# Hybrid block, one core: tiles that TensorE reads at one end of the SBUF, the rest at the other

## The chip, the core and the metric

The kernel runs on one core of a Trainium2 chip. A core has five engines with a queue each: TensorE (PE in the profile; its weight loads are PEld), VectorE (DVE), ScalarE (ACT), GpSimd (POOL) and SyncE (SP), which here only starts transfers. They share a 128-partition on-chip memory, the SBUF, and PE writes to a second one, the PSUM, in banks of 2 KB per partition. Each queue is worked in order; semaphores hold an instruction until others are done.

The metric is the device time of one call in microseconds (us), the median of several runs.

## The reference

One layer, for 1024 tokens of width 1024, all in float32:

```python
h = rms_norm(x, g_pre)
u = einsum('bsd,dn->bsn', h, w_in)             # 1024 x 8192: 10 blocks of 512, and 3*1024 merge logits
y_pool = pool_mixer(pool_v, ...) * silu(pool_g)     # causal means over 2, 4, 8, 16 tokens, then a 128x128 mix
y_conv = conv_mixer(conv_x, conv_gb, conv_gc, ...) * silu(conv_g)   # 3-tap causal convolution
y_sb = stick_breaking_attention(q, k, v) * silu(sb_g)               # 8 heads of 64
proj = einsum('bsnw,nwd->bsnd', branches, w_branch)  # three projections 512 -> 1024
merged = sum(sigmoid(merge) * proj, over the branches)
out = x + rms_norm(einsum('bsd,de->bse', merged, w_out), g_post)
```

In the attention a weight is sigmoid(logit) times the product of sigmoid(-logit) over all later keys, so each row needs a reversed running product (a scan) in place of a softmax.

## The kernel before, in words

Every operand of a product is held as two parts, a rounded high part and the rest (`hi`, `lo`), and a product is three matmuls: hi by hi, hi by lo, lo by hi. `split` (L72) makes the parts: a ScalarE copy (L73) and a subtraction on VectorE or GpSimd (L74). Weights are loaded in 128x512 pieces into `wraw` or `sraw`, split into the `w_hi` and `w_lo` tiles of the pool `wsp` (three of each, so up to two ahead), and used once.

Four stages follow each other.

1. To about 34 us: x is loaded, normed and transposed into `hh` and `hl`, four tiles each (two halves of the features by two halves of the tokens).
2. To about 332 us: the attention. `logits` (L366) multiplies queries with keys, takes two sigmoids (`sn`, `sp`, ScalarE), scans `sn` on VectorE (L386), and multiplies `sp` by the shifted `sn` on GpSimd (L388). `transposes` turns `sp` on PE, splits it into `wh` and `wl`; `values` (L408) multiplies with the values into `o`, adds a `low` half and writes `y_sb`. Between these steps `fillers` issues the blocks of the input product for the next heads (L189). The tile `tmp` takes the values before their transposition and the gates of this branch.
3. To about 936 us: everything else of the input product, in pairs of blocks by a seven-product scheme (`run_pair`, L564). It needs seven right-hand sides: three quarters of h as they are (`b11`, `b21`, `b22`), the quarter `b12` overwritten by a combination (`t4`), and three new combinations `t1`, `t2`, `t3`, each a pair of tiles (`t1h`, `t1l` and so on) of the pool `quarters`, built once by `build_quarters`. A product (L539) is 12 matmuls of 128x512. A pair takes the products b11, t2, b21, t3, t1, t4, b22 in this order, and there are 24 pairs. Between them stand the branch projections (`branch_proj`, L491; 24 matmuls per 128 outputs): of the attention first, with its parts in the pool `ysp` (L506), later of the other two with theirs in `ypp`. Partial sums are kept in DRAM (`proj_d`) and read back as `pr`; the merge gates and branch outputs are the tiles `g`, `sig`, `y`, `ph`, `pl` of the pool `gates`, the terms of a pair are `m1`, `u2`, `u3` of `tmps`.
4. To the end: the output product (L796), with the eight merged rows `m` as the stationary operand and the halves of w_out (`oh`, `wo`) moving, then the norm and the residual. The first four `m` were stored to DRAM and are read back (`taken_back`, L749) through the tiles `mr`; they go to the pool `fin`. The last four reuse `big`, the pool that held h.

A scheduler sets the order on each engine from the order of the code and its own estimates, and it inserts the waits. It also gives each pool its place: pools on the left are stacked upward from the low end of the SBUF, pools with `side="right"` downward from the high end, and a pool that is closed gives its room to later ones. With `reuse_waits="tile"` a tile that lies on old ones waits for the users of these alone. The right-hand stack of this build starts at byte 229,344 of a partition, which is 32 more than a multiple of 64; the left-hand tiles start at multiples of 64.

```python
bigp = op("big", KB)
tpool, close_t = pool_of("quarters", 6, side="right")
stp, close_stp = pool_of("stp", 2, side="right")
ysp, close_ysp = pool_of("ysp", 4, side="right")
held["m"] = op("fin", 1, side="right", reuse_waits="tile")
```

Of the kernel before, what the change touches and what calls it, by code (L numbers as in the profile page):

```python
# [8 lines left out]
F32 = mybir.dt.float32  # L9
# [5 lines left out]
P = 128  # L15
# [20 lines left out]
def hybrid_block_kernel(ctx, tc, x, g_pre, w_in, pool_w, pool_scale, conv_w, conv_b, w_branch, w_out, g_post, out):  # L36
# [17 lines left out]
    wraw = op("wraw", 3)  # L54
# [164 lines left out]
    ysb_pool = ysb_stack.enter_context(tc.tile_pool(name="ysb", bufs=4))  # L219
    qk_stack = ExitStack()  # L220
    qkp = qk_stack.enter_context(tc.tile_pool(name="qk", bufs=3))

    def tmp_tile():
        return qkp.tile([P, S], F32, tag="tmp", name="tmp", bufs=2)
# [96 lines left out]
    with tc.tile_pool(name="au", bufs=3) as au, \  # L321
            tc.tile_pool(name="wt", bufs=3) as wtp, tc.tile_pool(name="ps_z", bufs=2, space=PSUM) as ps_z, \
# [43 lines left out]
        def logits(p, s, i):  # L366
            n = (i + 1) * P
            q = ops["q", p][s]
            k, kl = ops["k", p][s]
            qs = slice(i * P, n)  # L370
            sp = au.tile([P, S], F32, tag="sp", name="sp", bufs=4)
            sn = au.tile([P, S], F32, tag="sn", name="sn", bufs=2)
            mid = (i + 1) // 2 * P if n > HALF else 0
            for c0, c1 in ((mid, n), (0, mid)):
                if c0 == c1:
                    continue
                w = c1 - c0
                z = ps_z.tile([P, HALF], F32, tag="z", name="z")
                nc.tensor.matmul(z[:, :w], q[:, qs], k[:, c0:c1], start=True, stop=False)  # L379
                if c1 == n:  # L380
                    nc.tensor.matmul(z[:, w - P:w], ident_r, mask_r, start=False, stop=False)
                nc.tensor.matmul(z[:, :w], q[:, qs], kl[:, c0:c1], start=False, stop=True)  # L382
                nc.scalar.activation(sn[:, c0:c1], z[:, :w], AF.Sigmoid, scale=-0.125)  # L383
                nc.scalar.activation(sp[:, c0:c1], z[:, :w], AF.Sigmoid, scale=0.125)  # L384
            rev = sn[:, 0:n][:, ::-1]
            nc.vector.tensor_tensor_scan(out=rev, data0=rev, data1=zeros.to_broadcast([P, n]), initial=1.0, op0=ALU.mult,  # L386
                                         op1=ALU.max)
            nc.gpsimd.tensor_tensor(out=sp[:, 0:n - 1], in0=sp[:, 0:n - 1], in1=sn[:, 1:n], op=ALU.mult)  # L388
            ops["w", p, s, i] = sp
# [18 lines left out]
        def values(p, s, i):  # L408
# [11 lines left out]
            low = au.tile([P, 2 * P], F32, tag="low", name="low", bufs=2)  # L420
# [76 lines left out]
    tpool, close_t = pool_of("quarters", 6, side="right")  # L497
# [7 lines left out]
    stp, close_stp = pool_of("stp", 2, side="right")  # L505
    ysp, close_ysp = pool_of("ysp", 4, side="right")  # L506
# [42 lines left out]
    held["raw"] = op("sraw", 5, reuse_waits="tile")  # L549
    held["sum"] = op("ssum", 3, reuse_waits="tile")  # L550
    for d in range(KB):
# [3 lines left out]
        if d % 2 == 0:  # L555
            build_quarters(d // 2)
    close_ysp()
    close_stp()
    tmps, close_tmps = pool_of("tmps", 1, side="right")
# [117 lines left out]
    gpool = op("gates", 4, reuse_waits="tile")  # L677

# [55 lines left out]
    def take_merged(d, ts, m):  # L734
        if d not in m_parts:
            o = (held["m"].tile([P, 2, S], F32R, tag="m", name="m", bufs=4) if d < 4
                 else bigp.tile([P, 2, S], F32R, tag="big", name="m"))
# [11 lines left out]
    def taken_back():  # L749

        for d in range(KB):
            if d < 4:
                m = held["m"].tile([P, S], F32, tag="mr", name="mr", bufs=2)
# [21 lines left out]
    close_tmps()  # L775
    close_t()
    held["m"] = op("fin", 1, side="right", reuse_waits="tile")
# [8 lines left out]
    fin = held["m"]  # L786
    gpost_sb = fin.tile([P, D], F32, tag="gpost", name="gpost_sb")
# [17 lines left out]
    def square(ps, var):  # L805
        junk = fin.tile([P, HALF], F32, tag="junk", name="junk")
# [92 lines left out]
```

## Time and profile before

| | us |
|---|---|
| median of 3 runs | 1033.36 (1031.94 to 1034.29) |
| profiled execution, its own time | 1032.51 |
| its span, first to last instruction | 1030.7 |
| outside the span | 1.8 |
| PE busy | 997.1, 4752 matmuls |
| mean granted TensorE clock | 0.997 of full |

The page of a profile lists the busy time of each engine, the chain of work that ended last, and the costliest groups of instructions by line. A group reads: line, engine, operation, written tile, read tiles, shapes, count, busy time, mean duration, idle time before, and what ended that idle time. In a matmul's row the moving operand stands first after the arrow and the stationary one second. The duration of a matmul runs to its modelled end, so matmuls overlap in such rows; what one costs in a row of them is the distance from one start to the next. In the chain a row reads: start, length, engine, written tile, line, count.

### The profile page before, as it was taken

What the parts mean: (1) busy time and instruction counts of PE and PEld (TensorE: products, weight loads), DVE (VectorE), ACT (ScalarE), POOL (GpSimd) and SP (SyncE); (2) the same over time, 40 slices, a digit from 0 to 9 for tenths busy, and PEclk for the clock granted to TensorE, in tenths of its full rate; (3) what the DMA queues carried; (4) which work ended last, traced back from release to release, by engine and by line L of the source; (5) the groups of instructions that cost most, each with busy time, mean ns of one, the idle gap of its engine ahead of it and who ended that gap; (6) DMA issues with size and microseconds to landing.
All of it is one profiled execution on the core that took longest, in us unless ns stands there. A gap on an engine that the chain in (4) does not pass through costs nothing.

```text
span 1030.7 us, 13275 instructions
## 1 busy us (share of the span) xinstructions
PE 997.1 (97%) x4752; PEld 825.0 (80%) x4752; DVE 636.5 (62%) x847; ACT 447.8 (43%) x871; POOL 453.0 (44%) x359
## 2 busy tenths in 40 slices
PE   4999999999998999999999999999999999999997
PEld 3788888888887788888888888888888888887886
DVE  6556766767776968889686685566333434465133
ACT  6557668668664553332232233343332322354111
POOL 3134543634564015455445444445555565556000
PEclk9999999999999999999999999999999999999999
DMA  6101000100101442322212224455434533256033
GB/s 227 60 21 35 28 22 22 41 21 21 31 22 31 163 153 62 98 66 72 83 52 72 82 62 163 153 191 167 133 126 125 209 112 120 65 186 223 1 123 123
DMA packets 43986, 97.09 MB, mean 94 GB/s; under 512 B 5264, under 2 KB 5520, under 8 KB 43920
## 3 DMA queue, kind: packets, MB, share of 16 engines
q1 hardware_dynamic: 43776, 95.71, 28.5%
q8 instruction: 38, 0.62, 0.2%
q10 hardware_dynamic: 144, 0.52, 0.1%
q14 instruction: 28, 0.23, 0.1%
HBM read 73.15 MB, written 23.07 MB: 93 GB/s over the span
## 4 chain that ended last, share of the span: by engine, by line
PE 84%; ACT 5%; DVE 4%; POOL 3%; issue 2%; DMA 2%; SPq 0%; POOLq 0%; DVEq 0%; ACTq 0%
PE g_ps L539 26%; PE q_ps L539 17%; PE g_ps L189 12%; PE pp L491 11%; PE o_ps L796 8%; PE o L418 3%; PE tp L404 2%; DVE sn L386 2%; PE z L382 1%; PE z L379 1%; POOL w_lo L74 1%; POOL sp L388 1%; ACT sn L383 1%; DMA xt<-in_x_dram 1%; ACT sp L384 1%
## 5 line engine op out<-in xcount | busy, mean ns | idle before, releaser
L74 POOL TENSOR_TENSOR w_lo<-s,w_hi 128x512 fp32r<-128x512 f32 x95 | 132.4, 1394 | 181.6 <-ACT w_hi L73 179.1
L388 POOL TENSOR_TENSOR sp<-sp,sn 128x127 f32<-128x127 f32 (+3 forms) x64 | 81.2, 1272 | 132.9 <-DVE sn L386 69.0
L74 POOL TENSOR_TENSOR w_lo<-s_raw,w_hi 128x512 fp32r<-128x512 f32 x70 | 94.2, 1346 | 96.5 <-ACT w_hi L73 92.3
L386 DVE TENSOR_TENSOR_SCAN sn<-sn,zeros 128x128 f32<-128x128 f32 (+3 forms) x64 | 100.5, 1574 | 48.3 <-ACT sn L383 45.5
L73 ACT CAST w_hi<-s 128x512 fp32r<-128x512 f32 x96 | 59.6, 621 | 136.0 <-PE g_ps L539 65.7
L73 ACT CAST w_hi<-s_raw 128x512 fp32r<-128x512 f32 x70 | 43.4, 620 | 132.5 <-PE g_ps L539 52.6
L189 PE MATMUL g_ps<-hh,w_hi 128*128 128x512 f32 x240 | 99.4, 414 | 0.3 <-ACT hh L285 0.3
L189 PE MATMUL g_ps<-hl,w_hi 128*128 128x512 f32 x240 | 94.5, 394 | 0.3 <-DVE hl L286 0.3
L189 PE MATMUL g_ps<-hh,w_lo 128*128 128x512 f32 x240 | 94.5, 394 | 0.0
L539 PE MATMUL g_ps<-hh,w_hi 128*128 128x512 f32 x236 | 92.6, 392 | 0.0
L539 PE MATMUL g_ps<-hh,w_lo 128*128 128x512 f32 x236 | 92.1, 390 | 0.0
L539 PE MATMUL g_ps<-hl,w_hi 128*128 128x512 f32 x236 | 91.8, 389 | 0.0
L74 POOL TENSOR_TENSOR w_lo<-w_raw,w_hi 128x512 fp32r<-128x512 f32 x44 | 67.6, 1535 | 53.1 <-ACT w_hi L73 53.1
L491 PE MATMUL pp<-yhi,w_lo 128*128 128x512 f32 x192 | 75.0, 392 | 0.7 <-DVE g L717 0.7
L491 PE MATMUL pp<-ylo,w_hi 128*128 128x512 f32 x192 | 75.0, 392 | 0.0
L491 PE MATMUL pp<-yhi,w_hi 128*128 128x512 f32 x192 | 74.9, 391 | 0.0
L383 ACT ACTIVATE sn<-z 128x384 f32<-128x384 f32 (+2 forms) x96 | 47.9, 499 | 29.7 <-PE z L382 20.4
L232 DVE TENSOR_TENSOR wl<-tp,wh 128x512 fp32r<-128x512 f32 (+2 forms) x96 | 50.4, 544 | 15.4 <-ACT wh L405 14.9
L539 PE MATMUL q_ps<-hh,w_hi 128*128 128x512 f32 x148 | 58.0, 392 | 0.0
L539 PE MATMUL q_ps<-hh,w_lo 128*128 128x512 f32 x148 | 57.9, 391 | 0.0
L539 PE MATMUL q_ps<-hl,w_hi 128*128 128x512 f32 x148 | 57.5, 389 | 0.0
L133 DVE TENSOR_TENSOR s<-s_raw 128x512 f32<-128x512 f32 x48 | 41.9, 873 | 23.4 <-POOL w_lo L74 22.8
(205 smaller groups left out, 2423.8 us busy)
## 6 DMA issues: line engine op xcount, KB each, us to landing
s_raw<-in_w_in_dram SPq DMA_DIRECT2D x96, 256.0 KB, 2.6
pr<-proj SPq DMA_DIRECT2D x48, 256.0 KB, 3.5
proj<-g SPq DMA_DIRECT2D x20, 512.0 KB, 3.0
w_raw<-in_w_in_dram SPq DMA_DIRECT2D x34, 256.0 KB, 2.6
w_raw<-in_w_branch_dram SPq DMA_DIRECT2D x24, 256.0 KB, 2.6
xt<-in_x_dram SPq DMA_DIRECT2D x8, 512.0 KB, 7.9
proj<-proj SPq DMA_DIRECT2D x8, 512.0 KB, 2.7
wo_raw<-in_w_out_dram SPq DMA_DIRECT2D x16, 256.0 KB, 3.3
```

Source lines behind the costliest of these rows:

```text
L73: nc.scalar.copy(hi, raw)
L74: eng.tensor_tensor(out=lo, in0=raw, in1=f32(hi), op=ALU.subtract)
L133: nc.vector.tensor_tensor(out=o, in0=a, in1=b, op=how)
L189: nc.tensor.matmul(ps, l[:, a], r[k // 4][t][:, k % 4, :], start=(n == 0), stop=(n == 3 * KB - 1))
L232: nc.vector.tensor_tensor(out=o, in0=a, in1=f32(b), op=ALU.subtract)
L383: nc.scalar.activation(sn[:, c0:c1], z[:, :w], AF.Sigmoid, scale=-0.125)
L386: nc.vector.tensor_tensor_scan(out=rev, data0=rev, data1=zeros.to_broadcast([P, n]), initial=1.0, op0=ALU.mult, op1=ALU.max)
L388: nc.gpsimd.tensor_tensor(out=sp[:, 0:n - 1], in0=sp[:, 0:n - 1], in1=sn[:, 1:n], op=ALU.mult)
L418: nc.tensor.matmul(o[:, cs], vc[:, j, s, :], wt[j // 4][:, j % 4, cs], start=(j == 0 and wt is wl), stop=(j == i and wt is wh))
L491: nc.tensor.matmul(pp, l[:, a], r[:, HALVES[t]], start=(n == 0), stop=(n == 3 * NB - 1))
L539: nc.tensor.matmul(bank, l[:, a], r[:, j, :], start=(n == 0), stop=(n == 11))
L796: nc.tensor.matmul(ps, l[:, a], r[:, es], start=(d == 0 and n == 0), stop=(d == KB - 1 and n == 2))
```

## The change

Pools move from one end of the SBUF to the other; the computation and the instructions on the five engines stay the same, but for one tile's name.

```diff
-    wraw = op("wraw", 3)
+    wraw = op("wraw", 3, side="right")
...
-    ysb_pool = ysb_stack.enter_context(tc.tile_pool(name="ysb", bufs=4))
+    ysb_pool = ysb_stack.enter_context(tc.tile_pool(name="ysb", bufs=4, side="right"))
...
+    highp = qk_stack.enter_context(tc.tile_pool(name="high", bufs=2, side="right"))
...
-        return qkp.tile([P, S], F32, tag="tmp", name="tmp", bufs=2)
+        return highp.tile([P, S], F32, tag="tmp", name="tmp")
...
-    with tc.tile_pool(name="au", bufs=3) as au, \
-            tc.tile_pool(name="wt", bufs=3) as wtp, tc.tile_pool(name="ps_z", bufs=2, space=PSUM) as ps_z, \
+    with tc.tile_pool(name="wt", bufs=3) as wtp, \
+            tc.tile_pool(name="au", bufs=4) as au, tc.tile_pool(name="ps_z", bufs=2, space=PSUM) as ps_z, \
...
-            sp = au.tile([P, S], F32, tag="sp", name="sp", bufs=4)
-            sn = au.tile([P, S], F32, tag="sn", name="sn", bufs=2)
+            sp = au.tile([P, S], F32, tag="sp", name="sp")
+            sn = highp.tile([P, S], F32, tag="sn", name="sn")
...
-            low = au.tile([P, 2 * P], F32, tag="low", name="low", bufs=2)
+            low = highp.tile([P, 2 * P], F32, tag="low", name="low")
...
-    tpool, close_t = pool_of("quarters", 6, side="right")
+    tpool = op("quarters", 6, reuse_waits="tile")
...
-    stp, close_stp = pool_of("stp", 2, side="right")
-    ysp, close_ysp = pool_of("ysp", 4, side="right")
+    ysp, close_ysp = pool_of("ysp", 4)
+    stp, close_stp = pool_of("stp", 2)
...
-    held["raw"] = op("sraw", 5, reuse_waits="tile")
-    held["sum"] = op("ssum", 3, reuse_waits="tile")
+    held["raw"] = op("sraw", 5, side="right", reuse_waits="tile")
+    held["sum"] = op("ssum", 3, side="right", reuse_waits="tile")
...
-    tmps, close_tmps = pool_of("tmps", 1, side="right")
+    gpool = op("gates", 4, side="right", reuse_waits="tile")
+    tmps = op("tmps", 1, side="right", reuse_waits="tile")
...
-    gpool = op("gates", 4, reuse_waits="tile")
...
-            o = (held["m"].tile([P, 2, S], F32R, tag="m", name="m", bufs=4) if d < 4
-                 else bigp.tile([P, 2, S], F32R, tag="big", name="m"))
+            o = tpool.tile([P, 2, S], F32R, tag="t", name="m") if d < 4 else bigp.tile([P, 2, S], F32R, tag="big", name="m")
...
+        back = tpool.tile([P, 2, S], F32, tag="t", name="back")
...
-                m = held["m"].tile([P, S], F32, tag="mr", name="mr", bufs=2)
+                m = back[:, d % 2, :]
...
-    close_tmps()
-    close_t()
-    held["m"] = op("fin", 1, side="right", reuse_waits="tile")
...
-    fin = held["m"]
-    gpost_sb = fin.tile([P, D], F32, tag="gpost", name="gpost_sb")
+    fin = op("fin", 1, reuse_waits="tile")
+    late = tpool.tile([P, 2, S], F32, tag="t", name="late")
+    gpost_sb, junk = late[:, 0, :], late[:, 1, 0:HALF]
...
-        junk = fin.tile([P, HALF], F32, tag="junk", name="junk")
```

The placements that the two builds give, in bytes of a partition; behind each the remainder by 64:

| tiles | read by PE as | before | after |
|---|---|---|---|
| `hh`, `hl` (and `oh`, `m` of rows 4 to 7) | moving (`m`: stationary) | 37,056 to 102,591 (0) | 30,912 to 96,447 (0) |
| `t1h` to `t3l` | moving | 180,192 to 229,343 (32) | 96,448 to 145,599 (0) |
| `yhi`, `ylo` of the attention (`ysp`) | moving | 126,944 to 159,711 (32) | 145,600 to 178,367 (0) |
| `yhi`, `ylo` of the other branches (`ypp`), `wo` | moving | 139,456 to 172,223 (0) | 145,600 to 178,367 (0) |
| `m` of rows 0 to 3 | stationary | 189,856 to 222,623 (32) | 104,640, 112,832, 129,216, 137,408 (0) |
| `w_hi`, `w_lo` | stationary | 24,768 to 37,055 (0) | 18,624 to 30,911 (0) |
| `sp` | stationary (transposes) | 172,224 (0) | 166,080 (0) |
| `tmp` | stationary (transposes) | 164,032 (0) | 188,384 (32) |
| `ph`, `pl` | moving (24 matmuls) | 127,168 (0) | 194,528 (32) |
| `sn` | no | 188,608 (0) | 196,576 (32) |
| `w_raw`, `s_raw`, `s`, `g`, `pr` | no | 18,624 to 139,455 (0) | 186,336 to 229,343 (32) |

All other operands of PE start at multiples of 64 in both builds.

The order on the engines stays but for a few places. On SyncE, at the start of the last stage, the merged rows are read back (`mr<-proj` before, `back<-proj` after; `wo_raw` is a piece of w_out, `w_raw` one of the branch weights, `gpost_sb` or `late` the post-norm's factors). Before:

```order
L84 DMA w_raw<-in_w_branch_dram 128x512
L754 DMA mr<-proj_3521 128x1024
L754 DMA mr<-proj_3522 128x1024
L743 DMA wo_raw<-in_w_out_dram 128x512 x2
L788 DMA gpost_sb<-in_post_norm_g_dram 128x1024
L754 DMA mr<-proj_3523 128x1024
L84 DMA w_raw<-in_w_branch_dram 128x512
L754 DMA mr<-proj_3524 128x1024
L686 DMA pr<-proj_3526 128x512
```

After:

```order
L84 DMA w_raw<-in_w_branch_dram 128x512
L755 DMA back<-proj_3525 128x1024
L755 DMA back<-proj_3526 128x1024
L755 DMA back<-proj_3527 128x1024
L755 DMA back<-proj_3528 128x1024
L743 DMA wo_raw<-in_w_out_dram 128x512
L787 DMA late<-in_post_norm_g_dram 128x1024
L743 DMA wo_raw<-in_w_out_dram 128x512
L84 DMA w_raw<-in_w_branch_dram 128x512
```

The four reads now stand together, ahead of the pieces of w_out. The first of them waits, after the change, for the last t2 product of stage 3, since `back` takes the place of `t2l`; before it waited for the last t1 product, whose `t1h` lay where `mr` comes.

On VectorE, the same place a little later: `m<-mr` or `m<-back` are the low parts of the merged rows read back, the rows of L585 (L588 after) the sums of the last pair of stage 3. Before:

```order
L585 TENSOR_TENSOR g<-q_ps,m_8258 128x512
L585 TENSOR_TENSOR u_8260<-q_ps,u_8259 128x512
L585 TENSOR_TENSOR u_8259<-g_ps,u_8259 128x512
L585 TENSOR_TENSOR g<-g_ps,u_8260 128x512 x2
L74 TENSOR_TENSOR m<-mr,m 128x1024
L585 TENSOR_TENSOR g<-g_ps,u_8259 128x512
L74 TENSOR_TENSOR m<-mr,m 128x1024
L717 TENSOR_TENSOR g<-pp,g 128x512
```

After:

```order
L588 TENSOR_TENSOR g<-q_ps,m_8262 128x512
L74 TENSOR_TENSOR m<-back,m 128x1024
L588 TENSOR_TENSOR u_8264<-q_ps,u_8263 128x512
L74 TENSOR_TENSOR m<-back,m 128x1024
L588 TENSOR_TENSOR u_8263<-g_ps,u_8263 128x512
L588 TENSOR_TENSOR g<-g_ps,u_8264 128x512
L74 TENSOR_TENSOR m<-back,m 128x1024
L588 TENSOR_TENSOR g<-g_ps,u_8264 128x512
L74 TENSOR_TENSOR m<-back,m 128x1024
L588 TENSOR_TENSOR g<-g_ps,u_8263 128x512
L718 TENSOR_TENSOR g<-pp,g 128x512
```

All four are now between the sums of the last pair, ahead of the first product with a projection (L717, L718 after); before, two were there and two among those products. ScalarE's casts of the same rows move with them.

On VectorE at the end of the attention, the low parts of the attention's output (`ylo`) and the first sums for the combinations (`q`). Before:

```order
L462 TENSOR_TENSOR ysb<-ysb,tmp 128x512
L515 TENSOR_TENSOR q<-hh_1_71,hl_1_75 128x512
L515 TENSOR_TENSOR q<-hh_1_73,hl_1_77 128x512
L74 TENSOR_TENSOR ylo<-ysb,yhi 128x1024
L74 TENSOR_TENSOR w_lo<-w_raw,w_hi 128x512
L74 TENSOR_TENSOR ylo<-ysb,yhi 128x1024 x3
```

After:

```order
L464 TENSOR_TENSOR ysb<-ysb,tmp 128x512
L74 TENSOR_TENSOR ylo<-ysb,yhi 128x1024 x3
L74 TENSOR_TENSOR w_lo<-w_raw,w_hi 128x512
L74 TENSOR_TENSOR ylo<-ysb,yhi 128x1024
L74 TENSOR_TENSOR w_lo<-w_raw,w_hi 128x512
L517 TENSOR_TENSOR q<-hh_1_71,hl_1_75 128x512
L517 TENSOR_TENSOR q<-hh_1_73,hl_1_77 128x512
```

Two sums have moved behind the four low parts; on ScalarE three `yhi` casts stand ahead of the next weight's cast, where it was one. In the attention itself the order on all engines is the same.

More of the change, by code (lines that the diff above doesn't have):

```diff
@@ L556, in hybrid_block_kernel @@
             build_quarters(d // 2)
+    close_stp()
     close_ysp()
-    close_stp()
-    tmps, close_tmps = pool_of("tmps", 1, side="right")
+    gpool = op("gates", 4, side="right", reuse_waits="tile")
+    tmps = op("tmps", 1, side="right", reuse_waits="tile")
     held["q"] = op("ps_q", 2, space=PSUM, reuse_waits="tile")
```

## The prediction

> **What bounds the kernel now.** I read the page's busy times first, then busy time by stage, then the chain of waits, then single matmuls.
>
> ```profile
> PE 997.1 (97%) x4752; PEld 825.0 (80%) x4752; DVE 636.5 (62%) x847; ACT 447.8 (43%) x871; POOL 453.0 (44%) x359
> core 0: us, PE busy (x) PEld busy (x) DVE busy (x) ACT busy (x) POOL busy (x), PEclk, DMA share, GB/s
> 34.00:332.00 298.00, 287.71 (x1635) 245.86 (x1634) 198.17 (x256) 195.92 (x441) 134.49 (x95) 1.00 0.09 27
> 332.00:936.00 604.00, 603.20 (x2621) 490.93 (x2621) 383.78 (x491) 212.09 (x344) 290.04 (x212) 1.00 0.37 120
> 936.00:1031.00 95.00, 88.41 (x408) 72.97 (x406) 30.07 (x59) 17.80 (x45) 17.30 (x18) 0.98 0.31 103
> ```
>
> TensorE is the bound. From 332 to 936 us it is busy 603.2 of 604.0 us at a granted clock of 1.00, and in the output stage until its last matmul. In such a stretch nothing that another engine does earlier shortens the kernel; only fewer matmuls or a shorter distance from one to the next does. So the question for a change of placement alone is whether that distance depends on where the operands lie. The chain says that it isn't the same everywhere:
>
> ```profile
> 337.92 44.88 PE pp L491 x192
> ...
> 399.40 5.56 PE q_ps L539 x24
> 404.96 8.36 PE g_ps L539 x36
> 413.32 1.36 PE mx L648 x6
> 414.68 5.44 PE q_ps L539 x24
> ...
> 711.98 10.88 PE pp L491 x48
> ...
> 935.94 86.21 PE o_ps L796 x389
> ```
>
> All of these but the mx and the last row are 128x512 matmuls without a pause. Per matmul: 44.88 / 192 = 233.75 ns in the attention's projections, 10.88 / 48 = 226.7 ns in the later ones at the same line L491. Products go b11, t2, b21, t3, t1, t4, b22 in each pair; the 24 matmuls at 414.68 are b22 and the next b11, 5.44 / 24 = 226.7 ns, and those at 399.40 are t2 and b21, 5.56 / 24 = 231.7 ns. Single matmuls show the same next to each other:
>
> ```profile
> 904.72 0.39 PE L539 MATMUL g_ps<-t1h,w_hi 128*128 128x512 f32 x1
> ...
> 907.52 0.40 PE L539 MATMUL g_ps<-hh,w_hi 128*128 128x512 f32 x1
> ...
> 910.27 0.39 PE L539 MATMUL g_ps<-hh,w_hi 128*128 128x512 f32 x1
> ...
> 912.99 0.39 PE L491 MATMUL pp<-yhi,w_lo 128*128 128x512 f32 x1
> ```
>
> The 12 of t1 take 2.80 us (233.3 ns each), the 12 of t4 after them 2.75, the 12 of b22 2.72 (226.7). The longer have an operand whose start is 32 past a multiple of 64 in the placement table (t1 to t3; yhi and ylo of the attention), the shorter have none. Two comparisons inside this trace take away other explanations. Depth in the SBUF is not it: the yhi and ylo of the attention, at 233.75, lie at bytes 126,944 to 159,711, those of the other branches, at 226.7, lie at 139,456 to 172,223, mostly the same bytes. Nor is it what the other engines do meanwhile: t and b products alternate every 2.7 us under the same load. t4 and b21 start at a multiple of 64 and still take a little more than 226.7 each time they follow a t product, as if the lag of the t product were worked off there; with it gone they should run like b22.
>
> **The change part by part.** All sums go against the profiled execution: span 1030.7, own time 1032.51, so 1.8 us outside the span; it lies 0.85 us under the median, 1033.36, and I carry the difference over to the median.
>
> *Right-hand quarters t1 to t3 to multiples of 64.* One pair is t2 to the next b11: 5.56 + 8.36 + 5.44 = 19.36 us for 84 matmuls without the mix (L648) between. At 226.7 ns it is 84 x 0.2267 = 19.04. The difference is 0.32 us, times 24 pairs: **-7.7 us**. Bounds: 0, and this whole sum.
>
> *The attention's yhi, ylo.* 44.88 - 192 x 0.2267 = **-1.4 us**; bounds 0 and -1.4.
>
> *Four merged rows m, here the stationary operand.* The output row holds 389 matmuls, 29 of them of half width:
>
> ```profile
> 1020.81 3.60 PE L796 MATMUL o_ps<-wo,m 128*128 128x256 f32 x29
> ```
>
> 3.60 / 29 = 0.12 us each. 86.21 - 360 x 0.2267 - 29 x 0.12 = 1.1, so **-1.1 us**, if a stationary operand off its 64 costs as a moving one does. The excess speaks for it, since no moving operand of this stage is off; bounds 0 and -1.1.
>
> *What moves the other way.* ph and pl become moving operands at remainder 32 in 24 matmuls (the mx row), tmp a stationary one in 32 transposes: 56 x 6.7 ns = **+0.4 us**; bounds 0 and +0.4.
>
> *Reading the merged rows back.* Before, the four reads and their splits came late and met the projections:
>
> ```profile
> 907.71 0.80 SPq L754 DMA_DIRECT2D mr<-proj  x2
> DMA to landing us min/median/max: 3.1/4.5/5.7
> L74 DVE TENSOR_TENSOR m<-mr,m x4: 1209/1312/1607, 912.0 to 923.5; 128x1024 fp32r<-128x1024 f32 x4
> PE pp L491 <- DVE g L717: 0.7, 1, 0.7
> 904.92 0.69 DVE L585 TENSOR_TENSOR u<-q_ps,u 128x512 f32<-128x512 f32 x1 [2.11 <-PE q_ps L539]
> 904.74 0.62 ACT L73 CAST w_hi<-s 128x512 fp32r<-128x512 f32 x1 [1.27 <-PE q_ps L539]
> ```
>
> At 932 us PE waited 0.7 us for VectorE's L717 to free a bank, behind a queue in which two of the splits stood. Now the reads wait for the last t2, about 900 us, and land 3.1 to 5.7 us later. Ahead of them in SP's queue stands one weight load as before; behind them wait w_out's pieces, needed after 936, and the weight of projection row 7, needed near 930. On VectorE the first split stands ahead of the sum at 904.92, and on ScalarE its cast ahead of the sigmoid and the weight at 904.74. Landed after 3.1 us, the cast (1.05) and the split (1.2) end at 905.4, 0.5 us late on an engine that idled 2.1 us just before. Landed after 5.7, they end at 908, 3 us late; the weight's parts then come at about 908, and PE uses them in b22 at 910.27. So the read stalls nothing even then, and the wait at 932 should go: **-0.7 us**; bounds -0.7 and +1 (a PE wait like the one before, in a new place).
>
> *End of the attention.* Four low parts ahead of two sums:
>
> ```profile
> 334.02 1.29 DVE L515 TENSOR_TENSOR q<-hh,hl 128x512 f32<-128x512 f32 x2
> 335.23 1.22 DVE L74 TENSOR_TENSOR ylo<-ysb,yhi 128x1024 fp32r<-128x1024 f32 x1
> 336.36 0.69 DVE L74 TENSOR_TENSOR w_lo<-w_raw,w_hi 128x512 fp32r<-128x512 f32 x1
> 336.96 3.49 DVE L74 TENSOR_TENSOR ylo<-ysb,yhi 128x1024 fp32r<-128x1024 f32 x3
> ```
>
> The low parts come 1.3 us sooner, the sums 6 us later; their combinations are first used after the projections, at 382. The moved weight serves the second projection row, at 337.92 + 5.6. Cost 0, hidden by PE's 192 matmuls. The other moves (wraw, s_raw, gates, tmps, proj) change addresses and a few waits for transfers long landed; nothing of PE hangs on them.
>
> *The other engines' operands.* This is the unknown. GpSimd has two rates in this trace:
>
> ```profile
> L719 POOL TENSOR_TENSOR g<-pr,g 128x512 f32<-128x512 f32 x24 | 31.9, 1332 | 10.2 <-DVE g L717 8.0 <-DMA pr<-proj 2.2
> L388 POOL TENSOR_TENSOR sp<-sp,sn 128x1023 f32<-128x1023 f32 x8 | 16.0, 1997 | 9.3 <-DVE sn L386 4.8 <-PE z L382 4.6
> L388 POOL TENSOR_TENSOR sp<-sp,sn 128x511 f32<-128x511 f32 x8 | 8.7, 1091 | 16.0 <-DVE sn L386 8.6 <-PE g_ps L189 4.9 <-ACT sp L384 2.5
> PE 84%; ACT 5%; DVE 4%; POOL 3%; issue 2%; DMA 2%; SPq 0%; POOLq 0%; DVEq 0%; ACTq 0%
> 310.62 2.39 POOL L358 TENSOR_TENSOR ysb<-ysb,tmp 128x1024 f32<-128x1024 f32 x1
> ```
>
> With both inputs at remainder 0 it takes 2.39 us for 1024 columns and about 1.3 for 512; L388, whose second input starts one element (4 bytes) further, takes 2.00 and 1.09. After the change that input is at remainder 36, and the raw weights of L74 at 32 beside parts at 0. No row shows such a pair. If L388 loses its lead, it costs 0.2 us per 512 columns, about 0.22 on its mean width of 575, 64 times: +14.2 us of GpSimd. If L74 gains it, the some 28 splits in the attention save 0.2 each, -5.6. GpSimd makes up 3% of the chain of 1031 us, 31 of its 453 us, so about 7% of such a sum reaches the end: +1.0 or -0.4. I take 0, since L388 keeps unequal remainders; bounds +14.2 and -5.6 for the whole of it.
>
> Sum: -7.7 - 1.4 - 1.1 + 0.4 - 0.7 = **-10.5 us**: 1022.0 for the profiled execution, 1022.9 for the median.
>
> The Trainium skill speaks against this sum. Its page "TensorE: Matmul & The Clock Gate", section "Back-to-back issue gap", gives the distance of isolated matmuls by width alone, about 216 ns for 512 columns, and "SBUF — State Buffer", section "Who interferes with whom", lets only the port pair of VectorE and GpSimd contend. By these rules no tile's place costs PE anything, and the sum would be 0. The trace disagrees, with 226.7 and 233 ns side by side at full clock; that this follows the address, and not something else about these tiles, it can't show.
>
> **The rivals.**
>
> *The distance does not follow the address.* What t1 to t3, the attention's y and four of the m share besides the address is the right-hand side itself. For it: no tile of the trace changes its place while it keeps its role. Against it: three kinds of tiles, moving and stationary, made by different code, show the same excess. Then only the wait at 932 goes: 1033.36 - 0.7 = 1032.7, no change. This is also what the skill's two rules above give.
>
> *PE runs into its feeders.* In the merge-gate pairs PE once already waited for a weight:
>
> ```profile
> 823.07 2.12 POOL L74 TENSOR_TENSOR w_lo<-s,w_hi 128x512 fp32r<-128x512 f32 x1 [3.93 <-ACT w_hi L73]
> POOL w_lo L74 <- ACT w_hi L73: 324.5, 170, 51.2
> ```
>
> If a load, whose time doesn't shrink, comes last in each of the 12 merge-gate pairs, their 12 x 0.32 = 3.8 us stay: 1026.7. Against it: GpSimd idles 324.5 us in all until ScalarE hands it a weight, which itself waits for PE to free a buffer; the supply follows PE.
>
> *GpSimd slows down in the attention* and the kernel ends slower. L388 stands between the scan and the transposes; at 2.39 us per 1024 it costs 14.2 us more. It decides once more than 10.5 + 2.1 us of these lie on the path, that is nine tenths; with all of them the time is 1022.9 + 14.2 = 1037.1. For it: PE had 298.0 - 287.7 = 10.3 us idle in that stage, so GpSimd is near. Against it: only 7% of its time is on the chain, and an unequal remainder stays unequal.
>
> **How the numbers follow.** Forecast 0.78: 1022.9, with its own range 1018.5 to 1025. Feeders 0.10: 1026.7. Address without effect 0.08: 1032.7. GpSimd slower 0.04: 1037.1. About 0.2%, 2 us here, is what a measurement of this kernel can tell from no change. Faster by more than that is the forecast and the feeders, 0.88; within it 0.08; slower 0.04. The low end takes most of GpSimd's -5.6 (1022.9 - 4.4), the high end the feeders with a part of GpSimd's loss: 1018.5 to 1028.5, which leaves out the last two cases.
>
> **What would show it.** In the chain of the changed kernel the pairs' rows of 24 and 36 matmuls should all read 226 to 228 ns per matmul, whether t or b; the 192 of the attention's projections 43.5 us; the output row 85.1. Stage 3 should last some 9.5 us less, the stage before it change by under 2 us. L388's row of 1023 columns tells GpSimd's case (1997 ns or about 2390), the wait of PE for L717 the read-back's. The prediction is wrong if t products still take 2.80 us, or if PE's busy share of stage 3 falls under 99%.

## The result, and the profile after

| | before | changed |
|---|---|---|
| median of the runs, us | 1032.70 (1031.94 to 1034.29, 4 runs) | 1022.37 (1021.45 to 1023.04, 4 runs) |
| span of the profiled execution, us | 1030.7 | 1020.1 |
| PE busy, us | 997.1 | 986.8 |

The ratio is 0.9897, with a 95% interval of 0.9880 to 0.9915: the changed kernel is faster by 10.3 us, or 1.0%. The forecast was 1022.9. The number came out; the experiments show that the rule behind it did not hold as it was put.

Busy time by stage of the changed kernel, with the limits of stage 3 moved by what it lost (columns: the stretch, its length, then busy time and instructions of PE, PE's weight loads, DVE, ACT, POOL, the granted clock, the DMA share and GB/s):

```profile
34.00:332.00 298.00, 288.13 (x1637) 246.33 (x1636) 198.21 (x256) 195.90 (x440) 134.38 (x95) 1.00 0.09 27
332.00:926.50 594.50, 593.67 (x2618) 491.40 (x2618) 380.14 (x489) 211.87 (x344) 290.89 (x213) 1.00 0.37 122
926.50:1020.10 93.60, 87.25 (x408) 73.11 (x406) 30.43 (x59) 17.70 (x45) 16.37 (x17) 0.98 0.31 103
```

PE is still busy all but 0.8 us of stage 3, 593.67 of 594.5 us, at a clock of 1.00 as before. It does the same matmuls in less time; the other engines run as many instructions as before. The chain of waits shows where (start, length, engine, written tile, line, count; L491, L539, L648 and L796 of before are L493, L541, L651 and L795 here):

```profile
337.49 43.52 PE pp L493 x192
381.01 2.72 PE g_ps L541 x12
...
397.33 5.44 PE q_ps L541 x24
402.77 8.16 PE g_ps L541 x36
410.93 1.40 PE mx L651 x6
412.33 5.46 PE q_ps L541 x24
...
926.40 85.04 PE o_ps L795 x389
```

Every product now takes 226.7 ns per matmul, t or b: the row of t2 and b21 is 5.44 where it was 5.56, that of t3, t1 and t4 8.16 where it was 8.36 (b22 and the next b11, behind the mix, read 5.46 where they read 5.44). The projections went from 233.75 to 43.52 / 192 = 226.7 ns. Only the mix reads more than before, 1.40 us for six where it was 1.36; its ph and pl are the moving operands that went to remainder 32.

The span splits by these rows (difference: after less before):

| piece | before | after | difference |
|---|---|---|---|
| up to the attention's projections | 337.92 | 337.49 | -0.43 |
| these projections | 44.88 | 43.52 | -1.36 |
| rest of stage 3 | 553.14 | 545.39 | -7.75 |
| output row | 86.21 | 85.04 | -1.17 |
| after it | 8.55 | 8.66 | +0.11 |
| span | 1030.7 | 1020.1 | -10.6 |

PE's wait for L717 is gone, and there is a new one, at 470 us. The waits of PE from 330 us on (us, times, longest) hold this row alone:

```profile
PE q_ps L541 <- POOL w_lo L74: 0.8, 1, 0.8
```

The timeline of the changed kernel there, of PE, ScalarE and GpSimd (start, duration, instruction, and in brackets the idle time before it with what ended it):

```profile
469.67 0.39 PE L541 MATMUL q_ps<-hl,w_hi 128*128 128x512 f32 x1
470.90 0.50 PE L541 MATMUL q_ps<-hh,w_lo 128*128 128x512 f32 x1 [0.83 <-POOL w_lo L74]
467.21 1.05 ACT L73 CAST ph<-pb 128x1024 fp32r<-128x1024 f32 x1 [5.28 <-DVE pb L673]
468.17 0.61 ACT L73 CAST w_hi<-s_raw 128x512 fp32r<-128x512 f32 x1
468.86 1.98 POOL L74 TENSOR_TENSOR w_lo<-s_raw,w_hi 128x512 fp32r<-128x512 f32 x1 [4.14 <-ACT w_hi L73]
```

The distance of the two matmuls is 1.23 us, so 1.0 us more than 0.227. ScalarE stood 5.28 us ahead of the cast of ph, which needs VectorE's pb; the cast of a weight is behind it in its queue, GpSimd makes the low part from that, and PE needs it. Before, the pairs were 0.3 us longer each and the weight came just in time. GpSimd's row of before ends at 472.96 us, and PE's matmul with this weight started at 473.02:

```profile
470.96 2.00 POOL L74 TENSOR_TENSOR w_lo<-s_raw,w_hi 128x512 fp32r<-128x512 f32 x1 [4.13 <-ACT w_hi L73]
```

### The profile page after: what moved, and what is told of

Its sections match the earlier page's. It is cut to its first block, busy times and chain, and to the rows that moved or that the text cites. A ratio compares the mean times of both kernels' runs of the same rounds, so it can differ in the third digit from the quotient of the medians.

```text
span 1020.1 us, 13279 instructions
## 1 busy us (share of the span) xinstructions
PE 986.8 (97%) x4752; PEld 826.1 (81%) x4752; DVE 633.3 (62%) x847; ACT 447.5 (44%) x871; POOL 452.9 (44%) x359
## 4 chain that ended last, share of the span: by engine, by line
PE 87%; DVE 4%; ACT 4%; POOL 2%; issue 2%; DMA 1%; POOLq 0%; SPq 0%; DVEq 0%; ACTq 0%
PE g_ps L541 27%; PE q_ps L541 18%; PE pp L493 13%; PE g_ps L189 12%; PE o_ps L795 8%; PE o L420 3%; PE tp L406 2%; DVE sn L388 2%; PE z L384 1%; PE z L381 1%; POOL sp L390 1%; ACT sn L385 1%; DMA xt<-in_x_dram 1%; DVE xt L275 1%; DVE wl L234 1%
## 5 line engine op out<-in xcount | busy, mean ns | idle before, releaser
L74 POOL TENSOR_TENSOR w_lo<-s,w_hi 128x512 fp32r<-128x512 f32 x95 | 133.4, 1405 | 173.9 <-ACT w_hi L73 171.2
L390 POOL TENSOR_TENSOR sp<-sp,sn 128x127 f32<-128x127 f32 (+3 forms) x64 | 81.0, 1270 | 132.7 <-DVE sn L388 64.0
L74 POOL TENSOR_TENSOR w_lo<-s_raw,w_hi 128x512 fp32r<-128x512 f32 x70 | 95.3, 1361 | 92.4 <-ACT w_hi L73 92.3
L541 PE MATMUL g_ps<-hh,w_hi 128*128 128x512 f32 x236 | 92.0, 390 | 0.0
L541 PE MATMUL g_ps<-hl,w_hi 128*128 128x512 f32 x236 | 91.9, 389 | 0.0
L541 PE MATMUL g_ps<-hh,w_lo 128*128 128x512 f32 x236 | 91.9, 389 | 0.0
L74 POOL TENSOR_TENSOR w_lo<-w_raw,w_hi 128x512 fp32r<-128x512 f32 x44 | 67.1, 1525 | 51.3 <-ACT w_hi L73 51.3
L493 PE MATMUL pp<-ylo,w_hi 128*128 128x512 f32 x192 | 74.8, 389 | 0.0
L493 PE MATMUL pp<-yhi,w_hi 128*128 128x512 f32 x192 | 74.8, 389 | 0.0
L493 PE MATMUL pp<-yhi,w_lo 128*128 128x512 f32 x192 | 74.8, 389 | 0.0
L541 PE MATMUL q_ps<-hh,w_lo 128*128 128x512 f32 x148 | 57.7, 390 | 0.8 <-POOL w_lo L74 0.8
L541 PE MATMUL q_ps<-hh,w_hi 128*128 128x512 f32 x148 | 57.7, 390 | 0.0
L541 PE MATMUL q_ps<-hl,w_hi 128*128 128x512 f32 x148 | 57.7, 390 | 0.0
```

The source lines that it names most:

```text
L74: eng.tensor_tensor(out=lo, in0=raw, in1=f32(hi), op=ALU.subtract)
L493: nc.tensor.matmul(pp, l[:, a], r[:, HALVES[t]], start=(n == 0), stop=(n == 3 * NB - 1))
L541: nc.tensor.matmul(bank, l[:, a], r[:, j, :], start=(n == 0), stop=(n == 11))
```

## The experiments

The time of the kernel before beside each is the median of its runs on the same chip. A time per matmul is a row of the chain (start, length, engine, written tile, line, count) divided by its count. The changed kernel's 1022.37 is the one from above.

### The address alone, without a move

The kernel before, with 32 unused bytes at the upper end; all right-hand tiles go down by 32 bytes.

```diff
-    const = op("const", 1)
+    const = op("const", 1); pad = op("pad", 1, side="right").tile([P, 8], F32, tag="pad", name="pad"); nc.vector.memset(pad, 0.0)
```

> The kernel before with one unused tile of 32 bytes at the upper end, so that its right-hand stack starts at a multiple of 64; no pool moves to the other end and no order changes. If the start address by 64 sets the matmuls' distance: t1 to t3, the attention's yhi and ylo and rows 0 to 3 of m all read 226.7 ns, -7.7 - 1.4 - 1.1 = -10.2 us against the kernel before, 1022.5 us; the wait of 0.7 us at the merged rows stays. If it was the right-hand side, the neighbours or the role of these tiles: no change, 1032.7, t products at 233.5 ns.

1023.43 us against 1032.2, ratio 0.9912 (0.9897 to 0.9928). Its chain, and behind it the waits of PE from 330 us on:

```profile
338.17 43.76 PE pp L491 x192
...
398.25 5.44 PE q_ps L539 x24
403.69 8.16 PE g_ps L539 x36
...
928.25 85.41 PE o_ps L796 x390
```

```profile
PE q_ps L539 <- POOL w_lo L74: 0.9, 1, 0.9
PE pp L491 <- DVE g L717: 0.8, 1, 0.8
```

8.8 us of the gain come without moving a pool from one end to the other: t products at the right-hand end read 226.7 ns too. That the distance does not follow the address is refuted. The read-back's wait for L717 stays, as expected, and the new wait for a weight is there as well, so it belongs to the shorter pairs and not to the moved pools. Two rows are a little long, 43.76 (227.9 ns) and 85.41. The second finds its reason below. In the first, PE's weight load waits 0.3 us for VectorE's `ylo` at about 339.5 us; it does so in the kernel before too, and not in the changed one, where the low parts stand ahead of the two sums.

### The address alone, with everything moved

The changed kernel, with 32 unused bytes ahead of the pool of t1 to t3 and 32 behind it.

```diff
-    ps_p = op("ps_p", 3, space=PSUM)
+    ps_p = op("ps_p", 3, space=PSUM); pada = op("pada", 1).tile([P, 8], F32, tag="pada", name="pada"); nc.vector.memset(pada, 0.0)
...
-    t4 = b12
+    t4 = b12; padb = op("padb", 1).tile([P, 8], F32, tag="padb", name="padb"); nc.vector.memset(padb, 0.0)
```

> The changed kernel with 32 unused bytes ahead of the pool of t1 to t3 and 32 behind it: on the same side and nearly the same bytes, t1 to t3 and rows 0 to 3 of m (which lie in this pool) start at remainder 32, all else as in the changed kernel. If the address counts: +7.7 for t1 to t3 and +1.1 for m, 1022.4 + 8.8 = 1031.2, a pair at 19.36 us, t products at 233.5 ns. If the place at the lower end made the gain: 1022.4.

1032.19 us against 1032.2, ratio 1.0000 (0.9991 to 1.0009). 32 bytes undo the whole change. Its chain:

```profile
338.69 43.96 PE pp L493 x192
...
399.23 5.56 PE q_ps L541 x24
404.79 8.36 PE g_ps L541 x36
...
913.84 22.00 PE pp L493 x96
935.83 86.83 PE o_ps L795 x389
```

The rows of t2, b21 and of t3, t1, t4 are to the hundredth those of the kernel before. That is the expected 7.7 us. But 1.0 us more was lost than expected, although the wait at 470 us is gone here (from 330 us on PE waits for nothing). The output row shows a part of it, 1.79 us longer than 85.04 and not 1.1, and the projections another: 43.96 / 192 = 229.0 ns, and 22.00 / 96 = 229.2, though yhi and ylo start at a multiple of 64 here (145,664). All that changed for them is that they lie 64 bytes further than in the changed kernel. A rule of 64 does not explain that.

### Everything off

The changed kernel, with 32 unused bytes in the first pool at the lower end, so that all left-hand tiles go up by 32.

```diff
-    const = op("const", 1)
+    const = op("const", 1); pad = const.tile([P, 8], F32, tag="pad", name="pad"); nc.vector.memset(pad, 0.0)
```

> The changed kernel with 32 unused bytes at the lower end: every left-hand tile, so moving and stationary operands of nearly all matmuls, starts at remainder 32. If each matmul pays once, whichever operand is off: 3720 matmuls of 512 columns by 6.7 ns = +25 us, 1047. If moving and stationary add up (6.7 and the 5.2 ns by which rows 0 to 3 of m differed): 3720 x 11.9 ns = +44 us, 1066, distances of about 238 ns. If the address has no effect: 1022.4.

1022.48 us against 1032.2, ratio 0.9905 (0.9891 to 0.9918). Its chain:

```profile
338.69 43.52 PE pp L493 x192
...
398.53 5.44 PE q_ps L541 x24
403.97 8.16 PE g_ps L541 x36
412.13 1.36 PE mx L651 x6
...
927.42 85.04 PE o_ps L795 x389
```

Neither of the two sums that the theory allowed, +25 and +44 us, came: nothing was lost, and the mix got its 1.36 back. This is where the theory of the prediction falls. Nearly every operand of PE starts at remainder 32 here, and every distance is 226.7 ns.

### One operand off, by other amounts

First the weights alone: w_hi 32 bytes into its tile, w_lo 16, in tiles 64 bytes longer.

```diff
-        hi = wsp.tile([P, HALF], F32R, tag="hi", name="w_hi")
-        lo = wsp.tile([P, HALF], F32R, tag="lo", name="w_lo")
+        hi = wsp.tile([P, HALF + 16], F32R, tag="hi", name="w_hi")[:, 8:8 + HALF]
+        lo = wsp.tile([P, HALF + 16], F32R, tag="lo", name="w_lo")[:, 4:4 + HALF]
```

> The changed kernel with only the stationary weights off: w_hi at remainder 32, w_lo at remainder 16, all moving operands at 0. If a stationary operand off its 64 costs as the rows of m did (232.6 against 227.4 ns), whatever the remainder: 3360 matmuls by 5.2 ns = +17.5 us, 1040, w_lo's distances like w_hi's. If 16 costs nothing, only w_hi's two thirds of them: +11.7, 1034. If only moving operands count: 1022.4.

1037.2 us against 1032.5, ratio 1.0043 (1.0029 to 1.0056): 14.8 us more than the changed kernel. Its chain:

```profile
339.58 44.70 PE pp L493 x192
...
401.01 5.57 PE q_ps L541 x24
406.58 8.36 PE g_ps L541 x36
...
941.88 85.04 PE o_ps L795 x389
```

Projections at 232.8 ns and the 36 at 232.2: a stationary operand off alone costs about what a moving one does. Since each longer tile puts the next one 64 bytes further, these rows are means over several starts of the weights. The output row, which doesn't use these tiles, is as in the changed kernel. The total lies half way between the two sums expected, and the rows do not part the two tiles.

Then the moving operands of the projections alone, by 16 bytes for the attention and by 4 for the other branches.

```diff
-        hi = pool.tile([P, S], F32R, tag="yhi", name="yhi")
+        hi = pool.tile([P, S + 16], F32R, tag="yhi", name="yhi")[:, 4:4 + S]
...
-            hi = ypp.tile([P, S], F32R, tag="yhi", name="yhi")
+            hi = ypp.tile([P, S + 16], F32R, tag="yhi", name="yhi")[:, 1:1 + S]
```

(and `ylo` likewise).

> The changed kernel with the moving operands of the branch projections off by other amounts: yhi and ylo of the attention at remainder 16, those of the other two branches at remainder 4. If any start off a multiple of 64 costs one more piece of 64 bytes (33 for 32 in a row of 2048 bytes): 192 projections of the attention 43.52 to 44.8 us, the chain's rows of 48 from 10.88 to 11.2, in all 576 x 6.7 ns = +3.9 us, 1026.3. If the cost grows with the remainder: +0.7 and +0.3 us, 1023.4. If only 32 counts: 1022.4.

1027.46 us against 1032.5, ratio 0.9947 (0.9932 to 0.9962). Its chain:

```profile
338.26 44.65 PE pp L493 x192
...
909.82 22.76 PE pp L493 x96
```

At 16 it is 232.6 ns, at 4 it is 22.76 / 96 = 237.1, more than at 32. So neither "one more piece of 64 bytes" nor a cost that grows with the remainder: a start 4 bytes off costs most.

### The new theory: where the two operands stand against each other

In every row at 226.7 ns so far the moving and the stationary operand start at the same place modulo 256. The placement table shows it for the two kernels: in the changed one t1h less w_hi is 96,448 - 18,624 = 77,824 = 304 x 256, yhi less w_hi 126,976 = 496 x 256, m less oh (104,640 - 30,912) 288 x 256; before, t1h less w_hi was 180,192 - 24,768 = 607 x 256 + 32. The projections at 229 in the second experiment stand 64 apart, the rows of m in the first (189,824, 32 less than before, against oh at 37,056) are 64 short of a multiple of 256, and with all moved by 32 the differences stay. To put it to a test against the old theory, the weights, t1 to t3, all y and wo were moved by 32, and h and oh left at remainder 0:

```diff
-    const = op("const", 1)
+    const = op("const", 1); pad = const.tile([P, 8], F32, tag="pad", name="pad"); nc.vector.memset(pad, 0.0)
...
-    wsp = op("wsp", 3)
+    wsp = op("wsp", 3); padw = op("padw", 1).tile([P, 56], F32, tag="padw", name="padw"); nc.vector.memset(padw, 0.0)
...
-    ps_p = op("ps_p", 3, space=PSUM)
+    ps_p = op("ps_p", 3, space=PSUM); padt = op("padt", 1).tile([P, 8], F32, tag="padt", name="padt"); nc.vector.memset(padt, 0.0)
```

> The changed kernel with w_hi and w_lo, t1 to t3, the y of all branches and wo at remainder 32, and hh, hl (so b11, b21, b22, t4) and oh at 0 as they were. New theory, that a matmul is short when its moving and its stationary operand start at the same place by 64 (or by 256): t products and projections at 226.7 ns, b products at 231 to 234, the reverse of the kernel before; 1152 matmuls of stage 3 and 768 of the attention, with 180 of the output, at most 2100 x 6.7 ns = +14 us, 1032 to 1036. Old theory, that each operand must itself start at a multiple of 64: every one of them has an operand off, so t products at 233.5 too, and about 3500 matmuls by 5 to 6.7 ns give 1040 to 1046.

1032.35 us against 1032.35, ratio 1.0002 (0.9993 to 1.0010): in the new theory's range, at its low end, and under the old one's. Its chain, and behind it the first matmuls of t1, t4 and b22 in the last pair, from the timeline of PE:

```profile
338.75 43.52 PE pp L493 x192
...
404.38 8.27 PE g_ps L541 x36
...
414.04 5.60 PE q_ps L541 x24
```

```profile
905.11 0.39 PE L541 MATMUL g_ps<-t1h,w_hi 128*128 128x512 f32 x1
...
907.83 0.40 PE L541 MATMUL g_ps<-hh,w_hi 128*128 128x512 f32 x1
...
910.63 0.40 PE L541 MATMUL g_ps<-hh,w_hi 128*128 128x512 f32 x1
```

It is the reverse of the kernel before. t1, at remainder 32 like the weights, takes 2.72 us (226.7 ns each); t4, at remainder 0, takes 2.80 (233.3). The row of b22 and b11 is 5.60 where it was 5.44 before and 5.46 in the changed kernel, and hh did not move modulo 256. So the distance follows the difference of the two starts, not either start.

How far equality must go was asked with t1 to t3 (and the m in their pool) 128 bytes further; the edit is that of the second experiment with 32 elements in each pad.

> The changed kernel with t1 to t3 (and rows 0 to 3 of m, which lie in the same pool) 128 bytes further, so at remainder 0 by 64 and by 128 but not by 256 against the weights. If equality by 64 or by 128 is enough: 226.7 ns in t products, 1022.4. If it must hold by 256 (as 64 gave 229.1 and 256 gave 226.7 in the projections): t products above 226.7 ns, near the 229 of an offset of 64, 864 x 2.4 ns = +2.1 us and +0.4 in the output, 1024.9.

1029.25 us against 1032.35, ratio 0.9967 (0.9955 to 0.9979). Its chain, and behind it the first matmuls of t1 and t4 in the last pair:

```profile
397.18 5.53 PE q_ps L541 x24
402.70 8.33 PE g_ps L541 x36
...
932.10 86.74 PE o_ps L795 x389
```

```profile
901.92 0.40 PE L541 MATMUL g_ps<-t1h,w_hi 128*128 128x512 f32 x1
...
904.72 0.39 PE L541 MATMUL g_ps<-hh,w_hi 128*128 128x512 f32 x1
```

t1 takes 2.80 us: 128 apart costs as much as 32, not the 2 ns of 64. Of the differences that were tried, only multiples of 256 are free:

| start of moving less start of stationary, modulo 256 | ns per matmul | row |
|---|---|---|
| 0 | 226.7 | the changed kernel; t1 to t3 in the first experiment, 607 x 256 |
| 4, and 4 past multiples of 64 | 237.1 | 22.76 / 96 |
| 16, and 16 past multiples of 64 | 232.6 | 44.65 / 192 |
| 32 | 233.3 | t1 before, 2.80 / 12 |
| 64 | 229.0 (233.3 in another row, see below) | 43.96 / 192 |
| 128 | 233.3 | 2.80 / 12 |
| 224 (32 less) | 233.3 | 5.60 / 24 |

The difference alone does not fix the size. In the second experiment wo stands 32 from rows 0 to 3 of m and 64 from rows 4 to 7, and the seven full blocks of tokens with wo take 39.20 us for their 168 matmuls, 233.3 ns each and not 229.0 for half of them. Nor is every even matmul short (even: its two operands a multiple of 256 apart) when uneven ones stand before it: t4 was so before, and the output row of the last run, 1.70 us longer than 85.04, holds more than 6.6 ns for each of the 180 matmuls that stand 128 apart.

Which two operands count shows in the starts of single matmuls with wo, which go through rows 0 to 7 of m block by block. Before, where rows 0 to 3 stand 32 off wo, it is 226 ns from the last matmul of row 3 to the first of row 4, and 235 from the last of row 7 to the first of row 0, in each of the seven blocks. In the run with the weights, t1 to t3 and wo at 32, where rows 4 to 7 are off, these two are 235 and 227. So in these rows a matmul is long when its moving operand stands uneven to the stationary operand of the next one, and not to its own. The t products fit this: before, it is 226.7 ns on average from the last matmul of h to the first of t2 or t3, and 235.8 from that one to the second.

### The rest aligned

The changed kernel with the 32 bytes at the upper end (the edit of the first experiment): ph, pl and tmp stand even with their partners too.

> The changed kernel with the same 32 bytes at the upper end: tmp, ph, pl, the raw weights and sn now start at multiples of 64 too, so no operand of PE is left off. If the address counts: the mx row of 6 matmuls goes from 1.40 to 1.36 us, 24 matmuls and 32 transposes give back 0.4 us, 1022.0. If it doesn't: 1022.4. GpSimd: L390 still reads its second input 4 bytes further, 1998 ns for 1023 columns as before by both.

1022.22 us against 1032.2, ratio 0.9903 (0.9889 to 0.9916). The mix goes back in its chain; behind it a row of GpSimd's groups (busy time, mean ns of one, then the idle time before and what ended it):

```profile
411.31 1.36 PE mx L651 x6
```

```profile
L390 POOL TENSOR_TENSOR sp<-sp,sn 128x1023 f32<-128x1023 f32 x8 | 16.0, 1998 | 9.3 <-DVE sn L388 4.8 <-PE z L384 4.6
```

In time it is not to be told from the changed kernel; 0.4 us were expected, and the runs cannot show so little. GpSimd's row of 1023 columns is unchanged, with its second input at remainder 4. PE's wait at 470 us is there too.

### GpSimd's price in the attention

The forecast took GpSimd at 0, with bounds of +14.2 and -5.6. sn was laid 28 bytes further, so that L390 reads it at a multiple of 64:

```diff
-            sn = highp.tile([P, S], F32, tag="sn", name="sn")
+            sn = highp.tile([P, S + 16], F32, tag="sn", name="sn")[:, 7:7 + S]
```

> The changed kernel with sn laid 28 bytes further, so that L390's shifted read starts at a multiple of 64 instead of 36 past one; nothing else moves. It prices the case in which GpSimd slows down in the attention. If the offset of 4 bytes gives the faster rate: L390 of 1023 columns from 1998 to about 2390 ns, +14.2 us of GpSimd in all; of these 7% on the path, +1.0, 1023.4, or nearly all of it, 1035 and more. If the rate doesn't hang on it: 1998 ns and 1022.4.

1026.12 us against 1032.5, ratio 0.9940 (0.9928 to 0.9952). L390 as a whole on the page of the changed kernel and on this run's, its widest form among GpSimd's groups, and then a row of the chain:

```profile
L390 POOL TENSOR_TENSOR sp<-sp,sn 128x127 f32<-128x127 f32 (+3 forms) x64 | 81.0, 1270 | 132.7 <-DVE sn L388 64.0
```

```profile
L390 POOL TENSOR_TENSOR sp<-sp,sn 128x127 f32<-128x127 f32 (+3 forms) x64 | 95.1, 1489 | 120.0 <-DVE sn L388 58.6
```

```profile
L390 POOL TENSOR_TENSOR sp<-sp,sn 128x1023 f32<-128x1023 f32 x8 | 19.1, 2386 | 4.6 <-DVE sn L388 4.6
```

```profile
341.72 43.52 PE pp L493 x192
```

L390 costs 95.1 us in place of 81.0, so +14.1 as the rival had it, and the attention's projections start at 341.72 instead of 337.49. The kernel is 3.7 us longer than the changed one: 27% of the sum reaches the end, not 7% and not nine tenths. VectorE's busy time grew in this run as well, from 633.3 to 639.1 us, and how much of the 3.7 comes by way of it is not shown.

The same with 20 bytes, so that the read starts at remainder 56 (`[:, 5:5 + S]`):

> The changed kernel with sn laid 20 bytes further, so that L390's second input starts at remainder 56 by 64: a multiple of 8, not of 16, 32 or 64. If a start off a multiple of 8 bytes is what gave GpSimd the faster rate: L390 of 1023 columns at 2386 ns and 1026.1, as with the start at 64. If any start off 64 gives it: 1998 ns and 1022.4.

1021.93 us against 1032.35, ratio 0.9896 (0.9882 to 0.9909). The same row of GpSimd's groups:

```profile
L390 POOL TENSOR_TENSOR sp<-sp,sn 128x1023 f32<-128x1023 f32 x8 | 16.0, 1995 | 9.3 <-DVE sn L388 4.8 <-PE z L384 4.6
```

It takes 1995 ns: a start at a multiple of 8 keeps the quicker rate. With the second input at 4, 36 and 56 it is 1995 to 1998, at 0 it is 2386. The first input starts at a multiple of 64 in all of these, so the runs cannot tell the second one's own start from its difference to the first.

And the raw weights 4 bytes further, in tiles 64 bytes longer, for `w_raw`, `s_raw`, `pw`, `wo_raw` and `s`:

```diff
-        raw = wraw.tile([P, HALF], F32, tag="raw", name="w_raw")
+        raw = wraw.tile([P, HALF + 16], F32, tag="raw", name="w_raw")[:, 1:1 + HALF]
```

> The changed kernel with the raw weights and their sums one element (4 bytes) further, remainder 36, so that GpSimd's split reads a first input 4 bytes off the second, as L390 does. If that offset gives GpSimd its faster rate: L74 of 512 columns from 1.35 to 1.4 us to about 1.1, 209 splits by 0.25 = 52 us less of GpSimd, and at most the wait of 0.8 us for a weight off the end: 1021.5 to 1022.4. If the rate hangs on the instruction and not on the offset: L74 unchanged, 1022.4.

1022.61 us against 1032.5, ratio 0.9904 (0.9890 to 0.9917). One of L74's groups on GpSimd:

```profile
L74 POOL TENSOR_TENSOR w_lo<-s_raw,w_hi 128x512 fp32r<-128x512 f32 x70 | 93.9, 1341 | 93.7 <-ACT w_hi L73 92.2 <-DMA w_raw<-in_w_branch_dram 1.4
```

L74 is unchanged (1361 ns in the changed kernel, 1346 before): a first input 4 bytes off its partner gains nothing. Whether it must be the second input, or L74 has no quicker rate at all, stays open; moving the second input, w_hi, would set PE's operands apart, and it wasn't tried.

### The new wait

The changed kernel with all operands of PE even, and the casts of ph on VectorE:

```diff
-            split(nxt[:, PAD:], ph, pl, nc.vector)
+            nc.vector.tensor_copy(ph, nxt[:, PAD:]); nc.vector.tensor_tensor(out=pl, in0=nxt[:, PAD:], in1=f32(ph), op=ALU.subtract)
```

> The changed kernel with the 32 bytes at the upper end (all operands of PE at equal places), and with the casts of ph on VectorE in place of ScalarE. If the wait of 1.0 us at 470 us stands because ScalarE holds that cast ahead of a weight's cast: it goes, 1022.2 - 1.0 = 1021.2. If the weight is late for another reason (GpSimd or the pair's sums on VectorE): the wait stays or moves, 1022.2 or more.

1020.77 us (1020.42 to 1021.43) against 1032.35, ratio 0.9885 (0.9872 to 0.9899). From 330 us on PE waits for nothing any more. Its chain:

```profile
337.72 43.52 PE pp L493 x192
...
925.24 85.04 PE o_ps L795 x389
```

From the first projection to the output it is 925.24 - 337.72 = 587.52 us, in the changed kernel 926.40 - 337.49 = 588.91, and in the one with the 32 bytes at the upper end, from which this one differs by the cast alone, 926.59 - 337.87 = 588.72. So ScalarE's cast was what held the weight. This version is the best of all; its distance from the changed kernel, 1.6 us, is under what a measurement of this kernel can tell from nothing, though the two ranges of runs do not meet.

## Why the prediction was right

**The bound.** It held. PE is busy 593.67 of 594.5 us in stage 3 after the change, and where the distances changed, the time changed by about their sum.

**t1 to t3, -7.7.** Right: 24 x (19.36 - 19.04), the rows read 5.44, 8.16 and 5.44 where no mix stands ahead, and putting the 32 bytes back in the second experiment brought 5.56 and 8.36 back. So is the lag of t4 and b21, which are now at 226.7 like the rest; what makes it stays open.

**The attention's y, -1.4, and four rows of m, -1.1.** Right: -1.36 and -1.17. About 0.1 of the first is PE's wait for `ylo`, which went with the new order and not with the address. That a stationary operand costs as a moving one was an assumption there; the weights put off alone showed it, 232.8 ns.

**The rule.** Here the working was right for this change and wrong as a rule. The step "moving operands to multiples of 64" should have read: to the same place modulo 256 as the weights. The two could not be told apart in the trace of before, where the weights all start at remainder 0 by 64 and every moving operand is at 0 or 32. They differ as soon as something else moves: the rule of 64 would have forecast 25 us or more lost for the kernel with everything at 32, which lost nothing, and nothing lost for t1 to t3 128 bytes further, which cost 7 us. In the change itself all pairs but the mix and the transposes of tmp came to differences that are multiples of 256, and that was not worked out.

**ph, pl and tmp, +0.4.** The part that shows is right: the mix is 1.40 instead of 1.36 in four rows, 0.16 us. The transposes of tmp cannot be read from these rows.

**The read-back, -0.7.** The wait for L717 went, as argued. But the feeders, a rival at 0.10, took about as much back at one place: 1.0 us at 470 us, in a pool pair and not in the merge-gate pairs where it was looked for. The prediction looked only at the weights that already came late; a cast held by another engine's work was not on the list. Three terms were not forecast: this wait, +1.0 us, a shorter one of before at 825 us that went, -0.4, and the end of the attention, -0.4, which is within what two profiled executions differ by: it ended between 337.1 and 338.7 us in the kernels that left it as it is. They nearly cancel, so it is in part luck that the sum of the table, -10.6, lies so near to -10.5.

**GpSimd, 0.** Right, since L390's second input stays off a multiple of 64 (1998 ns, before 1997). The price named for the other case was too low: of +14.1 us 3.7 reached the end and not 1.0. The share of the chain was the wrong measure. It was taken over the whole kernel; from 34 to 337 us alone L390 holds 3.3% of the changed kernel's chain, 10 of its 81 us or 12%, and that is too little as well. The chain holds only what already ended last, but that L390 simply joined it when it grew is not shown: in the run with the slower L390 it holds 2.6% there.

**The address without effect.** Refuted by the first two experiments. The Trainium skill, page "SBUF — State Buffer", section "Who interferes with whom", gives PE one read port for the moving operand and one for the weight load and calls them independent. The rows here do not agree: what a matmul takes hangs on where these two stand to each other, from 226.7 to 237.1 ns. That in the rows of wo it is the stationary operand of the next matmul that counts (235 against 226 ns) points to its load, which overlaps the matmul before it. What makes the two meet no run here shows; the time of the weight loads as such hardly differs (825.0 us before, 826.1 after, 828.9 with the weights off).

## What to carry to other kernels

Where PE is the bound, compare the distance of matmuls that differ only in their operands, and look up the start addresses of both: here 3% of a matmul hangs on whether moving and stationary operand start at the same place modulo 256, and an unused tile of 32 bytes gave 8.8 of the 10.3 us that the rebuilt layout gave. A rule read from one placement should be tried by moving both partners and then one. And an idle engine's sum should not be multiplied by its share of the chain: 27% came through where 7% stood in the chain.

## What had not been expected of the hardware

- The distance of 128x512 matmuls follows the difference of the operands' start addresses: 226.7 ns at multiples of 256, 229.0 at 64 (233.3 in one output row), 232.6 to 233.3 at 16, 32, 128 and 224, 237.1 at 4.
- In the output product the stationary operand that counts is that of the next matmul: before, 235 ns from an even row to an uneven one, 226 from an uneven row to an even one.
- Neither operand's own address matters: with all at remainder 32 it is 226.7, and with weights and t at 32 the products of h, at 0, became the long ones.
- GpSimd's product of two float32 inputs takes 2386 ns for 1023 columns when its second input starts at a multiple of 64, and 1995 to 1998 when it starts 4, 36 or 56 past one, with the first at a multiple of 64.
